# Layer 0's output product: its first half as seven block products

## The chip, the cores and the metric

The kernel runs on 1 core of one Trainium2 chip. The metric is the device time of one execution in microseconds (us). Before the change it is 828.9 us, the median of 3 runs (828.73 to 829.05). The profiled execution took 828.51 us, with a span of 826.8 us from its first to its last instruction.

## The reference, cut to what matters

Four residual layers over a sequence of 256 positions and 1024 channels, in float32. Layers 0 and 3 are mixer A:

```
def mixer_a(h, w_in, v_gain, w_s, b_s, w_out):
    proj = h @ w_in
    u = proj[..., :A_WIDTH]
    v = rms_norm(proj[..., A_WIDTH:2 * A_WIDTH], v_gain)
    z = proj[..., 2 * A_WIDTH:]
...
    mixed = jnp.einsum('gij,bcjgd->bcigd', ws, v) + b_s.T[None, None, :, :, None]
...
    y = u * mixed * jax.nn.silu(z)
    return y @ w_out
```

`A_WIDTH` is 2048, so `y` is 256 x 2048 and `w_out` is 2048 x 1024. Layer 1 is dilated attention, layer 2 multi-scale pooling. Each layer computes `x = x + mixer(rms_norm(x))`.

## The kernel before

**Three passes per product.** Every operand of a large product is a pair of float32r tiles, a rounded high part and the remainder as low part. `mm3` (L85) issues high x high, high x low and low x high, so three matmuls stand for one product. ScalarE rounds (`hi_of`, L91), VectorE subtracts (`lo_of`, L94).

**The weight stream.** All weights are one list of units of 128 x 1024 floats (two k-blocks of 128 rows by 512 columns, 512 KB). A unit is loaded by SyncE's queue into a raw buffer (`load_units`, tiles wr, wx, wy, xs), split by ScalarE (tile w48h for unit 48) and VectorE (w48l), and used by TensorE. Seven split pairs exist; in most stages the split of unit u+5 is written into the program while unit u is multiplied (`step` with AHEAD = 5). A raw buffer is loaded again as soon as VectorE has lowered its unit. An ordinary unit is used for both halves t = 0, 1 of the 256 positions: 2 k-blocks x 2 x 3 passes = 12 matmuls of 512 columns.

**Order.** Work beside the products is written as generators that `tick` advances; one tick passes per k-block, so two per ordinary unit. The order in which the generators emit is the program order of each engine, and each engine runs in that order. The numbers after `spawn(` and `yield` are delays in ticks.

**Layer 0** (`layer_a`): products v0 to v3 (units 0 to 15), then for n = 0 to 3 the products z (four units) and u (four units), units 16 to 47. After u of n, `y_task` multiplies on VectorE (L669 to L674), TensorE transposes y of each t (`yp`, L682) through one PSUM bank, ScalarE and VectorE split it into y0nh and y0nl. There is one `yp` bank, so the transposes of t = 1 start when VectorE has lowered those of t = 0. Then `proj_out` (L522) multiplies y by units 48 to 63 into four PSUM banks wo and adds them to x. In the figures below, unit 48 is the first unit of this output product.

**Seven products in layer 3.** Three of layer 3's z/u blocks (`SEVEN`) are already computed as seven block products after Strassen and Winograd in place of eight. Sums of weight quarters that this needs are made by POOL's DMA queue in DRAM (`sums_of_quarters`: copies at L188, accumulating transfers at L186), 16 transfers per block, spread over layers 0, 1 and 2; `JOBS = (19, 16)` says how many of the 48 are issued in layers 0 and 1. Sums of the left operand's quarters are made on VectorE (`sums_task`, L694). A product of this kind uses two units, each with one t only: 6 matmuls of 512 columns per unit (`product`, L720). The seven products' results are kept by ScalarE (`keep`, `minus`) and combined by VectorE.

**Next layer's constants.** `load_b` (L810) loads layer 1's masks and tables on POOL's queue into kcb, when layer 0's spatial weights are done with that tile, and 20 ticks later multiplies four small tables on VectorE (L827).

Of the kernel before, what the change touches and what calls it, by code (L numbers as in the profile page):

```python
# [17 lines left out]
P = 128  # L18
# [25 lines left out]
LAST_AHEAD = 3  # L44
WARM = 17
FILL = 4
SEVEN = (0, 2, 3)
JOBS = (19, 16)


@with_exitstack
def hybrid_trunk_kernel(ctx, tc, x, wts, norm_gainT, a_v_gain, a_wsT, a_bsT, b_gl, b_gv, c_scaleT,
# [92 lines left out]
    sums = {(n, j): dp.tile([4, P, UNIT], F32, name=f"sums{n}{j}") for n in SEVEN for j in range(2)}

    def seven_units(n):

        return n_units - 48 + 8 * n + (8 if n == 3 else 0)

    for n in reversed(SEVEN):
        z = seven_units(n)
        seq[z:z + 8] = [e[j] for e in (((n, 0, 0), (n, 0, 1)), (z, z + 1), (z + 6, z + 7), ((n, 3, 0), (n, 3, 1)),
                                       (z + 2, z + 3), ((n, 2, 0), (n, 2, 1)), ((n, 1, 0), (n, 1, 1)))
                        for j in range(2)]
    n_seq = len(seq)

    raw_users = {"wr": [-1] * RAW_BUFS, "xs": [-1], "wx": [-1], "wy": [-1]}

    def raw_place(i):  # L160

        return ("wr", "wr", "wx", "wr", "wy", "wr", "xs")[i % 7] if i >= n_units - 48 else "wr"

    def load_free():

# [22 lines left out]
                nc.gpsimd.dma_start(dst, src, max_dma_last_dim=UNIT)  # L188
            yield every

    def sum_jobs(n):

        z = seven_units(n)
        both = range(2)
        jobs = [(sums[n, j][i], wts[z + 2 * q + j], add) for i, q, add in
                ((0, 0, False), (2, 2, False), (0, 2, True), (2, 3, True)) for j in both]
        jobs += [(sums[n, j][3], sums[n, j][0], False) for j in both]
        jobs += [(sums[n, j][1], wts[z + 2 + j], False) for j in both]  # L200
        jobs += [(sums[n, j][3], wts[z + 6 + j], True) for j in both]
        jobs += [(sums[n, j][1], sums[n, j][3], True) for j in both]
# [319 lines left out]
    def proj_out(layer, nkt, yT, k0=0):  # L522


        acc = [[[(slice(0, HALF), pp(f"wo{layer}_{t}{n}"))] for n in range(2)] for t in range(2)]
        if layer == DEPTH - 1:

            acc[1][1] = [(slice(0, S), acc[1][1][0][1][:, :S]), (slice(S, HALF), atp(f"wo{layer}_b")[:, :S])]
        jt = (nkt - TAIL) // 2
        for j in range(k0 // 2, jt):  # L530
            for n in range(2):
                w = next_unit()
                for kk in range(2):
# [54 lines left out]
    def layer_a(layer, consts, pl, mid):  # L588
# [98 lines left out]
                    yield 1  # L687
            done.add(("y", layer, n))


        if layer == DEPTH - 1:
            smh, sml = pair(pl, [P, 4, 4, P], "sm", f"sm{layer}", 1)

        def sums_task():  # L694
            q = {}
            for k, t in ((1, 1), (0, 1), (0, 0), (1, 0)):
                d = q[k, t] = tmp("sz", f"sq{layer}{k}{t}", 4).rearrange("p (k c) -> p k c", c=P)
                hh, hl = (a[:, 4 * k:4 * k + 4, t * P:(t + 1) * P].bitcast(F32) for a in hcur)
                nc.vector.tensor_tensor(d, hh, hl, op=ALU.add)
                yield 1  # L700
            a11, a12, a21, a22 = q[0, 0], q[1, 0], q[0, 1], q[1, 1]
            for i, (d, a, b, op) in enumerate(((a22, a21, a22, ALU.subtract), (a21, a11, a21, ALU.subtract),
                                               (a11, a22, a11, ALU.subtract), (a12, a12, a11, ALU.add))):
                nc.vector.tensor_tensor(d, a, b, op=op)
                hi_of(smh[:, i], d)
                yield 1
                lo_of(sml[:, i], d, smh[:, i])
                yield 1
            done.add(("sums", layer))

        S_A21_A22, S_A11_A21, S_REST, S_A12_REST = range(4)

        def seven_products(n):

            need(("sums", layer))

            def sm(i):
                return lambda k: (smh[:, i, k], sml[:, i, k])

            def product(o, a, first):  # L720
                for j in range(2):
                    w = next_unit()
                    for kk in range(2):
                        k = 2 * j + kk
                        mm3(o, a(k), (w[0][:, kk], w[1][:, kk]), first and k == 0, k == 3)
                        step(kk, due=kk == 1)
# [104 lines left out]
    def layer_b(layer, consts, pl):  # L831
# [247 lines left out]
    def layer_c(layer, pl):  # L1079
# [285 lines left out]
```

## Time and profile before

| what | value |
| --- | --- |
| median of 3 runs | 828.9 us |
| the profiled execution, its span | 828.51 us, 826.8 us |
| TensorE (PE) busy | 821.1 us, 99% |
| VectorE (DVE) busy | 581.4 us, 70% |
| ScalarE (ACT) busy | 514.9 us, 62% |
| GpSimd (POOL) busy | 83.5 us, 10% |
| layer 0, products z and u | 51.7 to 147.4 us |
| layer 0, output product | 147.4 to 190.7 us |

Matmuls are pipelined: each is shown with 0.39 us, while the next one starts sooner, so a busy TensorE is not one at its peak, and the distance from start to start is the cost of a matmul. For VectorE too the distance of two starts is what an instruction takes in a full queue.

### The profile page before, as it was taken

How to read it: one execution, taken by the hardware profiler on the slowest of the kernel's cores; microseconds unless marked ns; L12 is line 12 of the kernel's file. 1: busy time of each engine (PE TensorE's matmuls, PEld its weight loads, DVE VectorE, ACT ScalarE, POOL GpSimd, SP SyncE). 2: the span in 40 equal slices, each digit the busy share in tenths (PEclk: the TensorE clock that was granted, in tenths of full speed). 3: DMA queues.
4: the chain of work that ended last, by engine and by line, in shares of the span. 5: the costliest groups of instructions: out<-in, count | busy, mean ns of one | idle time of the engine just before them, and what ended most of it. 6: DMA issues, size and time to landing. Idle time of an engine off the chain costs nothing.

```text
span 826.8 us, 12566 instructions
## 1 busy us (share of the span) xinstructions
PE 821.1 (99%) x4585; PEld 711.4 (86%) x4585; DVE 581.4 (70%) x958; ACT 514.9 (62%) x947; POOL 83.5 (10%) x117
## 2 busy tenths in 40 slices
PE   9999999999999999999999999999999999999998
PEld 7888888888988888888888889999988888888887
DVE  5876656646657667667668576897864799979692
ACT  7775444436668687688688567546643668656560
POOL 1113120000201021021011014020000000000000
PEclk9999999999999999999999999999999999999999
DMA  8879999562968357369447269999665378868661
GB/s 281 305 241 311 322 319 300 176 197 84 288 201 228 125 194 242 125 164 250 147 149 257 78 200 280 291 279 278 231 227 178 103 244 303 289 213 324 200 234 52
DMA packets 60895, 184.21 MB, mean 223 GB/s; under 512 B 5952, under 2 KB 19024, under 8 KB 60704
## 3 DMA queue, kind: packets, MB, share of 16 engines
q1 hardware_dynamic: 43440, 154.16, 53.9%
q0 software_dynamic: 17104, 28.96, 15.4%
q8 instruction: 36, 0.59, 0.3%
q10 hardware_dynamic: 288, 0.28, 0.1%
q14 instruction: 27, 0.22, 0.1%
HBM read 182.32 MB, written 26.21 MB: 252 GB/s over the span
## 4 chain that ended last, share of the span: by engine, by line
PE 97%; DVE 1%; DMA 1%; ACT 1%; issue 0%; POOL 0%; ACTq 0%
PE qk L87 5%; PE qk L89 5%; PE qk L88 5%; PE wo L87 5%; PE wo L89 5%; PE wo L88 5%; PE v L87 5%; PE v L89 5%; PE v L88 5%; PE z L89 2%; PE z L87 2%; PE u L87 2%; PE u L88 2%; PE z L88 2%; PE u L89 2%; PE cz L89 2%
## 5 line engine op out<-in xcount | busy, mean ns | idle before, releaser
L854 POOL TENSOR_TENSOR qr<-qm,m 128x8 f32<-128x8 f32 x12 | 19.9, 1658 | 215.4 <-DVE qm L853 215.4
L849 ACT ACTIVATE junk<-qk 128x128 bf16<-128x128 f32 x96 | 26.6, 277 | 7.3 <-PE qk L89 4.7
L858 ACT ACTIVATE qn<-qk,qr 128x128 f32<-128x128 f32 x96 | 27.5, 381 | 3.6 <-POOL qr L854 3.6
L307 POOL TENSOR_TENSOR r<-ms,m 128x1 f32<-128x1 f32 x6 | 4.3, 710 | 198.5 <-DVE ms L304 198.5
L325 ACT ACTIVATE hT<-hp,gT 128x128 fp32r<-128x128 f32 x48 | 13.0, 383 | 15.0 <-PE hp L321 15.0
L186 POOL DMA_DIRECT2D sums<-in_wts_dram x18 | 19.3, 1205 | 24.1 <-DMA sums<-in_wts_dram 13.1
L853 DVE TENSOR_SCALAR qm<-qs 128x8 f32<-128x8 f32 x12 | 2.1, 172 | 26.7 <-ACT junk L849 26.7
L551 DVE TENSOR_TENSOR x<-wo,x 128x512 f32<-128x512 f32 (+1 forms) x16 | 10.8, 672 | 13.4 <-PE wo L89 13.3
L849 ACT ACTIVATION_READ_ACCUMULATOR junk<-qk 128x1 f32 x96 | 18.9, 197 | 0.0
L330 DVE SCALAR_TENSOR_TENSOR hT<-hp,gT,hT 128x128 fp32r<-128x128 f32 x48 | 13.5, 343 | 7.4 <-ACT hT L325 7.4
L299 ACT ACTIVATE junk<-x 128x512 bf16<-128x512 f32 x16 | 10.2, 639 | 10.1 <-DVE x L551 9.9
L948 ACT ACTIVATE p<-p,rl 128x384 f32<-128x384 f32 (+1 forms) x16 | 11.5, 769 | 4.8 <-DVE rl L947 4.8
L879 PE MATMUL qt<-ident,qn 128*128 128x128 f32 x96 | 14.4, 272 | 0.0
L871 DVE TENSOR_TENSOR rb<-qn,kcb 128x32 f32<-128x32 f32 x96 | 13.7, 184 | 0.0
L879 PEld LDWEIGHTS qt<-ident,qn 128*128 128x128 f32 x96 | 11.7, 140 | 2.3
L607 DVE TENSOR_TENSOR vv<-v,kc 128x512 f32<-128x512 f32 x16 | 10.7, 686 | 4.0 <-ACT junk L605 3.7
L669 DVE SCALAR_TENSOR_TENSOR sz<-u,m,sz 128x512 f32<-128x512 f32 x8 | 6.0, 746 | 10.3 <-PE u L89 10.3
L944 ACT ACTIVATE p<-p,nb 128x768 f32<-128x768 f32 x8 | 7.5, 937 | 7.6 <-DVE nb L943 7.6
L188 POOL DMA_DIRECT2D sums<-in_wts_dram x18 | 12.1, 716 | 0.3 <-issue 0.3
L867 DVE TENSOR_TENSOR ra<-qn,kcb 128x64 f32<-128x64 f32 x48 | 10.6, 220 | 1.1 <-ACT qn L858 0.4
L626 POOL TENSOR_TENSOR vr<-vme,m 128x1 f32<-128x1 f32 x4 | 2.8, 716 | 73.5 <-DVE vms L622 73.5
L979 PE MATMUL pt<-ident,p 128*128 128x128 f32 x48 | 9.9, 274 | 0.0
(2965 smaller groups left out, 3359.3 us busy)
## 6 DMA issues: line engine op xcount, KB each, us to landing
wr<-in_wts_dram SPq DMA_DIRECT2D x251, 512.0 KB, 4.6
sums<-in_wts_dram POOLq DMA_DIRECT2D x36, 512.0 KB, 11.8
wr<-sums SPq DMA_DIRECT2D x19, 512.0 KB, 4.6
sums<-sums POOLq DMA_DIRECT2D x12, 512.0 KB, 8.5
wx<-in_wts_dram SPq DMA_DIRECT2D x7, 512.0 KB, 5.1
wy<-in_wts_dram SPq DMA_DIRECT2D x7, 512.0 KB, 5.3
wx<-sums SPq DMA_DIRECT2D x3, 512.0 KB, 5.4
kc<-in_a_wsT_dram POOLq DMA_DIRECT2D x2, 512.0 KB, 7.6
```

The lines of the kernel that those rows point to most:

```text
L87: nc.tensor.matmul(out_ap, lh[0], rh[0], start=start, stop=False, skip_group_check=True)
L88: nc.tensor.matmul(out_ap, lh[0], rh[1], start=False, stop=False, skip_group_check=True)
L89: nc.tensor.matmul(out_ap, lh[1], rh[0], start=False, stop=stop, skip_group_check=True)
L186: nc.gpsimd.dma_start(dst, src, accum_op=ALU.add, max_dma_last_dim=UNIT)
L188: nc.gpsimd.dma_start(dst, src, max_dma_last_dim=UNIT)
L325: nc.scalar.activation(h_parts(layer)[0][:, k, t * P:(t + 1) * P], pt[:, k % 4], AF.Copy, scale=gT[:, layer, k:k + 1])
L330: nc.vector.scalar_tensor_tensor(hTl, pt[:, k % 4], gT[:, layer, k:k + 1], hTh.bitcast(F32), op0=ALU.mult, op1=ALU.subtract)
L849: nc.scalar.activation(junk[:, :HD], ov[t][:, h], AF.Square, accum_out=ssq[t][:, h:h + 1])
L854: nc.gpsimd.tensor_tensor(rqs, ms, m05_row[:, :8], op=ALU.pow)
L858: nc.scalar.activation(qn[t][:, h], ov[t][:, h], AF.Copy, scale=rq[t][:, h:h + 1])
L871: nc.vector.tensor_tensor(rb[:, hs, s0:s0 + 16], qn[t][:, hs, s1:s1 + 16], c, op=ALU.mult)
L879: nc.tensor.transpose(pts[t][:, h], qn[t][:, h], ident)
```

## The change

**The block products.** The first 8 of the 16 units of layer 0's output product (y's blocks 0 and 1, that is k-blocks 0 to 7) become seven block products of two units: 14 units of 6 matmuls (units 48 to 61) in place of 8 units of 12. The other half stays as it was (units 62 to 69). The seven results go into banks xw, yw, zw, ww and are added to x straight from PSUM by VectorE, seven adds of 128 x 512 (`add`). Banks xw and zw collect more than one product: xw is added to x after its first product, then takes the second, is subtracted, takes the third, is subtracted and added; zw is added, takes a second product, is added again. So each later product of a bank waits for the add before it.

**The sums.** Four sums of weight quarters come from 16 more transfers on POOL's queue, 64 in all: 19 in layer 0, 24 in layer 1, 21 in layer 2. Layer 0's begin with this block and are written into the program before `load_b`. Four sums of y's quarters are made by VectorE (`left_sums`) during z and u of n = 2, in the idle tiles wx and wy, and split by both engines: 8 adds, 4 roundings, 4 subtractions.

**The postponed parts.** In layer 0 the transposes of y come 4 ticks after `y_task`'s products in place of 2, and `load_b` starts 48 ticks later.

```diff
-SEVEN = (0, 2, 3)
-JOBS = (19, 16)
+BLOCKS = {("wo", 0): 48, ("zu", 0): -48, ("zu", 2): -32, ("zu", 3): -16}
+JOBS = (19, 24)
...
+        order = (3, 0, 2, 6, 1, 5, 4) if b[0] == "zu" else (0, 1, 3, 6, 2, 5, 4)
+        seq[z:z + 8] = [quarters[q][j] for q in order for j in range(2)]
...
+        return ("wr", "wr", "xs", "wr", "wr", "wx", "wy")[(i - out_raw) % 7] if out_raw <= i < out_raw + 14 else "wr"
...
+    def part_product(o, a, first):
+
+        for j in range(2):
+            w = next_unit()
+            for kk in range(2):
+                k = 2 * j + kk
+                mm3(o, a(k), (w[0][:, kk], w[1][:, kk]), first and k == 0, k == 3)
+                step(kk, due=kk == 1)
...
+    def proj_seven(layer, yT, smh, sml):
+
+
+        def add(t, n, o, op=ALU.add):
+            xh = xt[t][:, n * HALF:(n + 1) * HALF]
+            nc.vector.tensor_tensor(xh, xh, o, op=op)
+            yield 1
...
+        xb = pp(f"xw{layer}")
+        part_product(xb, quarter(0, 0), True)
+        spawn(add(0, 0, xb), 1)
+        yb = pp(f"yw{layer}")
+        part_product(yb, quarter(1, 0), True)
+        spawn(add(0, 0, yb), 1)
+        need(("sums", layer))
+        zb = pp(f"zw{layer}")
+        part_product(zb, sum_tile(smh, sml, S_A21_A22), True)
+        spawn(add(1, 1, zb), 1)
+        part_product(xb, sum_tile(smh, sml, S_REST), False)
+        spawn(add(0, 1, xb, ALU.subtract), 1)
+        part_product(zb, sum_tile(smh, sml, S_A12_REST), False)
+        spawn(add(0, 1, zb), 1)
+        part_product(xb, sum_tile(smh, sml, S_A11_A21), False)
+        spawn(add(1, 1, xb, ALU.subtract), 1)
+        spawn(add(1, 0, xb), 1)
+        wb = pp(f"ww{layer}")
+        part_product(wb, quarter(1, 1), True)
+        spawn(add(1, 0, wb), 1)
...
+            if layer == 0 and n == 0:
+                spawn(sums_of_quarters(jobs[:JOBS[0]], 3, 29))
...
-        if layer == 0:
-            spawn(sums_of_quarters(jobs[:JOBS[0]], 4, 6))
+        def y_sums():
+
+            while ("y", layer, 1) not in done:
+                yield 1
+            room = [wx[:, 0], wx[:, 1], wy[:, 0], wy[:, 1]]
...
+            if n == 2 and ("wo", layer) in BLOCKS:
+                spawn(y_sums(), 4)
...
-            spawn(y_task(n, proj_tok(f"u{layer}{n}"), us))
-
-        proj_out(layer, 16, get, KT if layer == DEPTH - 1 else 0)
+            spawn(y_task(n, proj_tok(f"u{layer}{n}"), us, 4 if late(layer) else 2))
+
+        if ("wo", layer) in BLOCKS:
+            proj_seven(layer, get, smh, sml)
+        proj_out(layer, 16, get, KT if layer == DEPTH - 1 or ("wo", layer) in BLOCKS else 0)
...
-                    spawn(sums_of_quarters(jobs[JOBS[0]:sum(JOBS)], 10, 5))
+                    spawn(sums_of_quarters(jobs[JOBS[0]:sum(JOBS)], 7, 5))
...
-        spawn(sums_of_quarters(jobs[sum(JOBS):], 7, 4))
+        spawn(sums_of_quarters(jobs[sum(JOBS):], 5, 4))
...
-        spawn(load_b())
+        spawn(load_b(), 48)
```

The order of the instructions moves on VectorE at three places. The first is the stretch of layer 0 from n = 2 on, up to the lowering of y's block 2 for t = 0 (y02l). VectorE, before:

```order
L95 TENSOR_TENSOR w39l<-wr_944,w39h 128x1024
L95 TENSOR_TENSOR w40l<-wr_962,w40h 128x1024
L95 TENSOR_TENSOR w41l<-wr_999,w41h 128x1024
L95 TENSOR_TENSOR w42l<-wr_1024,w42h 128x1024
L95 TENSOR_TENSOR w43l<-wr_1044,w43h 128x1024
L95 TENSOR_TENSOR w44l<-wr_1062,w44h 128x1024
L669 SCALAR_TENSOR_TENSOR sz_1064<-u_0_1068,m_77,sz_1064 128x512
L674 SCALAR_TENSOR_TENSOR yy_1160<-mx_1104,bs_267,sz_1064 128x256 x2
L669 SCALAR_TENSOR_TENSOR sz_1066<-u_1_1069,m_77,sz_1066 128x512
L674 SCALAR_TENSOR_TENSOR yy_1164<-mx_1111,bs_267,sz_1066 128x256 x2
L95 TENSOR_TENSOR w45l<-wr_1087,w45h 128x1024
L95 TENSOR_TENSOR y02l<-yp_1186,y02h 128x4x128
```

VectorE, changed, the end of the same stretch (sm0h and sm0l are the parts of the sums of y's quarters):

```order
L605 TENSOR_TENSOR wx<-wy,wx 128x512
L97 TENSOR_TENSOR sm0l<-wx,sm0h 128x512
L97 TENSOR_TENSOR w44l<-wr_1061,w44h 128x1024
L752 SCALAR_TENSOR_TENSOR sz_1063<-u_0_1067,m_79,sz_1063 128x512
L757 SCALAR_TENSOR_TENSOR yy_1171<-mx_1109,bs_269,sz_1063 128x256 x2
L752 SCALAR_TENSOR_TENSOR sz_1065<-u_1_1068,m_79,sz_1065 128x512
L757 SCALAR_TENSOR_TENSOR yy_1175<-mx_1116,bs_269,sz_1065 128x256 x2
L605 TENSOR_TENSOR wx<-wx 128x512
L97 TENSOR_TENSOR sm0l<-wx,sm0h 128x512
L97 TENSOR_TENSOR w45l<-wr_1088,w45h 128x1024
L97 TENSOR_TENSOR w46l<-wr_1124,w46h 128x1024
L97 TENSOR_TENSOR y02l<-yp_1220,y02h 128x4x128
```

The eight adds and four lowerings of the sums now stand between y01l and y02l, two of them and w46l between the products of y and y02l.

The second place is the start of the output product. VectorE, before, after the last products of y:

```order
L95 TENSOR_TENSOR w53l<-wr_1281,w53h 128x1024
L95 TENSOR_TENSOR y03l<-yp_1382,y03h 128x4x128
L95 TENSOR_TENSOR w54l<-wr_1313,w54h 128x1024
L95 TENSOR_TENSOR y03l<-yp_1407,y03h 128x4x128
L95 TENSOR_TENSOR w55l<-wr_1332,w55h 128x1024
L95 TENSOR_TENSOR w56l<-wr_1350,w56h 128x1024
```

VectorE, changed, at the same place (x<-x,xw is the add of a product to x):

```order
L97 TENSOR_TENSOR w53l<-wx,w53h 128x1024
L97 TENSOR_TENSOR w54l<-wy,w54h 128x1024
L629 TENSOR_TENSOR x<-x,xw_1386 128x512
L97 TENSOR_TENSOR w55l<-wr_1281,w55h 128x1024
L97 TENSOR_TENSOR w56l<-wr_1305,w56h 128x1024
L97 TENSOR_TENSOR y03l<-yp_1432,y03h 128x4x128
L629 TENSOR_TENSOR x<-x,yw_1409 128x512
L97 TENSOR_TENSOR w57l<-wr_1338,w57h 128x1024
L97 TENSOR_TENSOR w58l<-wr_1356,w58h 128x1024
L97 TENSOR_TENSOR y03l<-yp_1463,y03h 128x4x128
L629 TENSOR_TENSOR x<-x,zw_1441 128x512
L97 TENSOR_TENSOR w59l<-wr_1374,w59h 128x1024
```

The adds of the products now stand among the splits; a unit here means half as many matmuls as before.

The third place is the end of the seven products, units 61 to 66. VectorE, before:

```order
L95 TENSOR_TENSOR w61l<-wr_1471,w61h 128x1024
L95 TENSOR_TENSOR w62l<-wr_1489,w62h 128x1024
L95 TENSOR_TENSOR w63l<-wr_1508,w63h 128x1024
L95 TENSOR_TENSOR w64l<-wr_1526,w64h 128x1024
L95 TENSOR_TENSOR w65l<-wr_1544,w65h 128x1024
L95 TENSOR_TENSOR w66l<-wr_1562,w66h 128x1024
```

VectorE, changed:

```order
L97 TENSOR_TENSOR w61l<-wy,w61h 128x1024
L97 TENSOR_TENSOR w62l<-wr_1421,w62h 128x1024
L905 TENSOR_TENSOR kcb<-kcb 128x192 x4
L629 TENSOR_TENSOR x<-x,zw_1441 128x512
L97 TENSOR_TENSOR w63l<-wr_1439,w63h 128x1024
L97 TENSOR_TENSOR w64l<-wr_1470,w64h 128x1024
L629 TENSOR_TENSOR x<-x,xw_1386 128x512 x2
L97 TENSOR_TENSOR w65l<-wr_1484,w65h 128x1024
L97 TENSOR_TENSOR w66l<-wr_1517,w66h 128x1024
L629 TENSOR_TENSOR x<-x,ww_1548 128x512
```

The four table products of the next layer (kcb) and four adds have come in. The last add, x<-x,ww, frees the bank that the ordinary products take for wo_11, from the second group of three matmuls of unit 63 on.

More of the change, by code (lines that the diff above doesn't have):

```diff
@@ L144, in hybrid_trunk_kernel, with first_of @@
     seq = list(range(n_units))
[L145 to L155, printed above, removed]
+    sums = {(b, j): dp.tile([4, P, UNIT], F32, name=f"sums{b[0]}{b[1]}{j}") for b in BLOCKS for j in range(2)}
+    def first_of(b):
+        return BLOCKS[b] % n_units
+    for b in sorted(BLOCKS, key=first_of, reverse=True):
+        z = first_of(b)
+        quarters = [(z, z + 1), (z + 2, z + 3), (z + 6, z + 7)] + [((b, i, 0), (b, i, 1)) for i in range(4)]
+        order = (3, 0, 2, 6, 1, 5, 4) if b[0] == "zu" else (0, 1, 3, 6, 2, 5, 4)
+        seq[z:z + 8] = [quarters[q][j] for q in order for j in range(2)]
     n_seq = len(seq)
+    more_raw = seq.index((("zu", 0), 0, 0))
+    out_raw = first_of(("wo", 0))
     raw_users = {"wr": [-1] * RAW_BUFS, "xs": [-1], "wx": [-1], "wy": [-1]}
     def raw_place(i):
-        return ("wr", "wr", "wx", "wr", "wy", "wr", "xs")[i % 7] if i >= n_units - 48 else "wr"
+        if i >= more_raw:
+            return ("wr", "wr", "wx", "wr", "wy", "wr", "xs")[(i - more_raw) % 7]
+        return ("wr", "wr", "xs", "wr", "wr", "wx", "wy")[(i - out_raw) % 7] if out_raw <= i < out_raw + 14 else "wr"
     def load_free():
@@ L189, in sums_of_quarters, with sum_jobs @@
             yield every
-    def sum_jobs(n):
-        z = seven_units(n)
+    def sum_jobs(b):
+        z = first_of(b)
         both = range(2)
-        jobs = [(sums[n, j][i], wts[z + 2 * q + j], add) for i, q, add in
+        jobs = [(sums[b, j][i], wts[z + 2 * q + j], add) for i, q, add in
                 ((0, 0, False), (2, 2, False), (0, 2, True), (2, 3, True)) for j in both]
[L199 to L202, printed above, removed]
+        jobs += [(sums[b, j][3], sums[b, j][0], False) for j in both]
+        jobs += [(sums[b, j][1], wts[z + 2 + j], False) for j in both]
+        jobs += [(sums[b, j][3], wts[z + 6 + j], True) for j in both]
+        jobs += [(sums[b, j][1], sums[b, j][3], True) for j in both]
         return jobs
@@ L522, in proj_out, with bank @@
     def proj_out(layer, nkt, yT, k0=0):
-        acc = [[[(slice(0, HALF), pp(f"wo{layer}_{t}{n}"))] for n in range(2)] for t in range(2)]
+        acc = [[[], []], [[], []]]
+        def bank(t, n):
+            if not acc[t][n]:
+                acc[t][n].append((slice(0, HALF), pp(f"wo{layer}_{t}{n}")))
+        if ("wo", layer) not in BLOCKS:
+            for t in range(2):
+                for n in range(2):
+                    bank(t, n)
         if layer == DEPTH - 1:
@@ L535, in proj_out @@
                     for t in range(2):
+                        bank(t, n)
                         for cs, o in acc[t][n]:
@@ L571, in proj_out, with left_sums @@
                 tick()
+    S_A21_A22, S_A11_A21, S_REST, S_A12_REST = range(4)
+    def left_sums(name, quarter, place, smh, sml, key):
+        q = {}
+        for k, t in ((1, 1), (0, 1), (0, 0), (1, 0)):
+            d = q[k, t] = place(f"sq{name}{k}{t}").rearrange("p (k c) -> p k c", c=P)
+            hh, hl = (a.bitcast(F32) for a in quarter(k, t))
+            nc.vector.tensor_tensor(d, hh, hl, op=ALU.add)
+            yield 1
+        a11, a12, a21, a22 = q[0, 0], q[1, 0], q[0, 1], q[1, 1]
+        for i, (d, a, b, op) in enumerate(((a22, a21, a22, ALU.subtract), (a21, a11, a21, ALU.subtract),
+                                           (a11, a22, a11, ALU.subtract), (a12, a12, a11, ALU.add))):
+            nc.vector.tensor_tensor(d, a, b, op=op)
+            hi_of(smh[:, i], d)
+            yield 1
+            lo_of(sml[:, i], d, smh[:, i])
+            yield 1
+        done.add(key)
@@ L688, in y_task, with h_quarter @@
             done.add(("y", layer, n))
-        if layer == DEPTH - 1:
+        if layer == DEPTH - 1 or ("wo", layer) in BLOCKS:
             smh, sml = pair(pl, [P, 4, 4, P], "sm", f"sm{layer}", 1)
[L694 to L711, printed above, removed]
+        def h_quarter(k, t):
+            return (a[:, 4 * k:4 * k + 4, t * P:(t + 1) * P] for a in hcur)
         def seven_products(n):
@@ L717, in sm @@
             def sm(i):
[L718 to L726, printed above, removed]
+                return sum_tile(smh, sml, i)
+            product = part_product
             def minus(o, name):
@@ L788, in get, with place, y_quarter @@
             return yT[k // 4][0][:, k % 4, sl], yT[k // 4][1][:, k % 4, sl]
-        if layer == 0:
-            spawn(sums_of_quarters(jobs[:JOBS[0]], 4, 6))
+        def y_sums():
+            while ("y", layer, 1) not in done:
+                yield 1
+            room = [wx[:, 0], wx[:, 1], wy[:, 0], wy[:, 1]]
+            def place(name):
+                return room.pop()
+            def y_quarter(k, t):
+                return (a[:, :, t * P:(t + 1) * P] for a in yT[k])
+            yield from left_sums(layer, y_quarter, place, smh, sml, ("sums", layer))
         for n in range(4):
+            if n == 2 and ("wo", layer) in BLOCKS:
+                spawn(y_sums(), 4)
             if layer == DEPTH - 1 and n == 3:
                 proj_half(layer, KT, get)
-            if layer == DEPTH - 1 and n in SEVEN:
+            if layer == DEPTH - 1 and ("zu", n) in BLOCKS:
                 seven_products(n)
@@ L1208, in hybrid_trunk_kernel @@
     box = {}
-    jobs = [e for n in SEVEN for e in sum_jobs(n)]
+    jobs = [e for b in BLOCKS for e in sum_jobs(b)]
     def after_ws():
-        spawn(load_b())
+        spawn(load_b(), 48)
     with tc.tile_pool(name="L0", bufs=1, reuse_waits="tile") as pl:
```

9 lines of the change are left out of this document (8 added, 1 removed).

## The prediction
> **What bounds the kernel now.** I read the page first: the busy shares, then the chain of work that ended last by engine.
>
> ```profile
> PE 821.1 (99%) x4585; PEld 711.4 (86%) x4585; DVE 581.4 (70%) x958; ACT 514.9 (62%) x947; POOL 83.5 (10%) x117
> PE 97%; DVE 1%; DMA 1%; ACT 1%; issue 0%; POOL 0%; ACTq 0%
> ```
>
> TensorE is on the chain for 97%. Next the view of waits for TensorE alone, all of its rows (total, times, longest):
>
> ```profile
> PE warm L291 <- DVE wx L65: 1.1, 1, 1.1
> PE hp L321 <- DVE xs L315: 0.5, 1, 0.5
> PE v L429 <- ACT hT L404: 0.3, 1, 0.3
> PE xb L87 <- ACT n L730: 0.3, 1, 0.3
> ```
>
> TensorE waits 2.2 us in all, nowhere in the stages that change. Then busy times by stage (span, then PE, PEld, DVE, ACT, POOL, granted clock, DMA share, GB/s); the rows are n = 2, n = 3 and the output product of layer 0:
>
> ```profile
> 98.50:123.00 24.50, 24.50 (x119) 20.51 (x118) 14.29 (x17) 10.49 (x12) 5.54 (x7) 1.00 1.10 332
> 123.00:147.40 24.40, 24.40 (x118) 20.41 (x118) 14.20 (x17) 10.49 (x12) 0.46 (x1) 1.00 0.90 288
> 147.40:190.70 43.30, 43.30 (x197) 35.77 (x197) 24.16 (x28) 17.05 (x20) 0.56 (x1) 1.00 0.53 170
> ```
>
> TensorE is full at granted clock 1.00; VectorE has 10 us free in n = 2 and 19 us in the output product. So a matmul removed is time removed, while VectorE keeps up with what is put on it.
>
> **Removed: 12 matmuls.** TensorE's timeline from u into the output product:
>
> ```profile
> 146.77 0.39 PE L87 MATMUL u<-w47h,hT 128*128 128x512 f32 x1
> ...
> 149.94 0.39 PE L89 MATMUL wo<-w48h,y00l 128*128 128x512 f32 x1
> ```
>
> These are the first and the last of 15 starts, so a matmul costs 3.17 / 14 = 0.2264 us. 8 units x 12 = 96 matmuls become 14 x 6 = 84: **-2.72 us**. An ordinary unit lasts 2.72 us, a seven-product unit 1.36.
>
> **What VectorE's additions cost.** Its timeline in a full queue (layer 3's first block):
>
> ```profile
> 697.09 1.22 DVE L95 TENSOR_TENSOR w232l<-wr,w232h 128x1024 fp32r<-128x1024 f32 x1
> 698.22 1.22 DVE L95 TENSOR_TENSOR w233l<-wx,w233h 128x1024 fp32r<-128x1024 f32 x1
> ...
> 707.43 0.68 DVE L758 TENSOR_TENSOR p<-yb,p 128x512 f32<-128x512 f32 x1
> 708.03 1.22 DVE L95 TENSOR_TENSOR w239l<-wr,w239h 128x1024 fp32r<-128x1024 f32 x1
> ```
>
> From start to start a split takes 1.14 us, an operation on 512 columns 0.60; the last of a queue ends 1.22 or 0.69 after its start. So each starts 0.08 or 0.09 before the one ahead of it is shown to end; that without this overlap VectorE would be later is the last rival. [...]
>
> The multiplication of y, the four table products, and the round trips with ScalarE are shown by these:
>
> ```profile
> 146.97 0.75 DVE L669 SCALAR_TENSOR_TENSOR sz<-u,m,sz 128x512 f32<-128x512 f32 x1 [3.90 <-PE u L89]
> ...
> 150.12 1.22 DVE L95 TENSOR_TENSOR w53l<-wr,w53h 128x1024 fp32r<-128x1024 f32 x1
> 151.44 0.69 DVE L95 TENSOR_TENSOR y03l<-yp,y03h 128x512 fp32r<-128x512 f32 x1
> 152.39 1.22 DVE L95 TENSOR_TENSOR w54l<-wr,w54h 128x1024 fp32r<-128x1024 f32 x1 [0.26 <-ACT w54h L92]
> ```
>
> ```profile
> 89.75 1.16 DVE L827 TENSOR_TENSOR kcb<-kcb 128x192 f32<-128x192 f32 x4
> 90.82 1.22 DVE L95 TENSOR_TENSOR w34l<-wr,w34h 128x1024 fp32r<-128x1024 f32 x1
> ```
>
> ```profile
> 658.32 0.69 DVE L607 TENSOR_TENSOR vv<-v,kc 128x512 f32<-128x512 f32 x1 [0.73 <-ACT junk L605]
> 658.92 1.48 DVE L95 TENSOR_TENSOR v30l<-vv,v30h 128x512 fp32r<-128x512 f32 x2
> 659.04 0.63 ACT L92 ACTIVATE v30h<-vv 128x512 fp32r<-128x512 f32 x1 [0.24 <-DVE vv L607]
> ```
>
> The products of y take 3.15 us, the tables 1.07. An operation, its rounding on ScalarE and its lowering take 1.39 us from start to start: 658.32 to the second lowering, which starts 0.69 before its end at 660.40. A split behind a lowering that waited for ScalarE starts 0.95 later (151.44 to 152.39), since ScalarE rounds in turn. So one sum of quarters with the split behind it costs 1.39 + 0.95 + 1.14 = 3.48 us.
>
> **Wait A: y's sums hold the second transposes of n = 2.** They start when y's block 1 is lowered, and the transposes of t = 1 need y02l of t = 0 behind them.
>
> ```profile
> 106.28 0.69 DVE L95 TENSOR_TENSOR y01l<-yp,y01h 128x512 fp32r<-128x512 f32 x1 [1.04 <-ACT y01h L92]
> ```
>
> ```profile
> 129.20 0.60 PE L682 MATMUL yp<-ident,yy 128*128 128x128 f32 x4
> ```
>
> Both move 2 ticks, one ordinary unit, later: y01l ends at 109.69, the transposes would start at 131.92. VectorE's queue between: four adds and two splits (2.40 + 2.28, to 114.4), three sums with a split (10.44, to 124.85), the products of y (3.15, to 128.0), the fourth sum with a split (3.48, to 131.5), w46l (1.14), y02l (0.69): 133.3. TensorE waits **1.4 us**. Postponing moves both ends alike, so it saves nothing here. Behind this wait in TensorE's queue stands only z, whose units are ready. The bounds are 0, if VectorE finds 1.4 us, and 2.7, if the 15 operations that follow another without a round trip each took their full 1.22 or 0.69 before the next starts (15 x 0.085 = 1.3).
>
> **Wait B: the last add frees a bank too late.** Count from TensorE's start of unit 48, where the products of y begin at -0.48 as before (147.45 against 146.97). Ahead of x<-x,ww stand, by the order: the products of y 3.15, the 14 splits w53l to w66l 15.96, seven adds 4.20, two lowerings of y 1.20, the tables 1.07, in sum 25.58. So x<-x,ww runs from 25.10 to 25.79. TensorE would need its bank after 14 units (19.02), two groups of transposes, unit 62 (2.72) and three matmuls (0.68). What transposes and a restart after a wait cost:
>
> ```profile
> 125.76 0.39 PE L89 MATMUL z<-w40h,hT 128*128 128x512 f32 x1
> 125.99 0.60 PE L682 MATMUL yp<-ident,yy 128*128 128x128 f32 x4
> 126.34 0.48 PE L87 MATMUL z<-w41h,hT 128*128 128x512 f32 x1
> 126.66 0.40 PE L88 MATMUL z<-w41l,hT 128*128 128x512 f32 x1
> ```
>
> ```profile
> 703.46 0.39 PE L89 MATMUL yb<-w233h,hT 128*128 128x512 f32 x1
> 704.11 0.50 PE L87 MATMUL xb<-w234h,sm3h 128*128 128x512 f32 x1 [0.27 <-ACT n L730]
> 704.44 0.39 PE L88 MATMUL xb<-w234l,sm3h 128*128 128x512 f32 x1
> ```
>
> Transposes add 0.45 (125.76 to 126.66 is 0.90 for two matmul steps of 0.45), a restart 0.10. So the need is at 23.32, and TensorE loses 25.79 - 23.32 + 0.10 = **2.6 us**. Part falls earlier: x<-x,zw ends at 12.6, and unit 56 needs that bank at 11.8; but the end is set by VectorE's queue alone, so earlier waits are inside the 2.6. The bounds are 0 and 4.6 (2.6, and 0.085 on some 24 operations). Behind the waiting matmul stand only the ordinary units; VectorE catches up there at 1.14 us of work per 2.72.
>
> **Edits at nothing.** Six more splits on ScalarE: it is busy 17.05 of 43.3 us above. Sixteen more transfers: layers 1 and 2 carried 29, now 45, and TensorE waited for none; bounded by one blocking POOL ahead of a norm for the 10.62 us it once waited, which five units of split weights (13.6 us) cover:
>
> ```profile
> 104.86 1.05 POOL L186 DMA_DIRECT2D sums<-in_wts_dram  x1 [10.62 <-DMA sums<-sums]
> ...
> 120.55 1.00 POOL L186 DMA_DIRECT2D sums<-sums  x1 [3.91 <-issue]
> ```
>
> `load_b` loads later, but 20 ticks still lie between it and the tables; without its transfers ahead the sums come sooner.
>
> **Sum.** 828.51 (profiled) - 2.72 + 1.4 + 2.6 = 829.8; on the median, 0.4 higher, 828.9 + 1.3 = 830.2. A comparison here can tell 0.2%, 1.7 us.
>
> **Rivals.**
>
> *The waits do not come (faster).* Layer 3's blocks have as full a VectorE, 23.32 of 24.00 and 21.98 of 23.00 us, and TensorE idles 0.27 and 0:
>
> ```profile
> 690.00:714.00 24.00, 23.73 (x110) 19.42 (x109) 23.32 (x27) 19.88 (x27) 1.73 (x2) 1.00 0.91 314
> 734.00:757.00 23.00, 23.00 (x112) 19.27 (x111) 21.98 (x25) 16.20 (x20) 0.00 (x0) 1.00 0.76 275
> ```
>
> With their worst loss (0.42 + 0.11 at 704) it is 828.9 - 2.72 + 0.53 = 826.7. Against it: there ScalarE frees the banks, here VectorE does, behind the splits. 14 in 100.
>
> *Late weights make wait B longer (slower).* w66's buffer is free when w62l ends at 17.75; a median landing and a split on ScalarE make it 17.75 + 4.6 + 1.06 = 23.4, and VectorE reaches w66l at 23.96.
>
> ```profile
> wr<-in_wts_dram SPq DMA_DIRECT2D x251, 512.0 KB, 4.6
> ```
>
> ```profile
> ACT w28h L92 <- DMA wr<-in_wts_dram: 5.0, 1, 5.0
> ```
>
> Beyond a landing of 5.2 us each microsecond is lost; ScalarE once waited 5.0 for one, among POOL's transfers. With 2 us late: 832.2. 12 in 100.
>
> *The sums come late.* SyncE's queue reaches them with w52 near 137 and holds all loads behind. Before, the first block's last transfer was issued at 120.55, and load_b's transfers no longer stand ahead of it. Ten microseconds late, less 6.8 of ready units, gives 833.4. 3 in 100.
>
> *VectorE's operations do not overlap.* Wait A grows by 1.3 and B by 2.0, their upper bounds: 833.5. Against it: the starts above. 2 in 100.
>
> **How the numbers follow.** 69 in 100 for the forecast, 829 to 831.4; about 47 of these within 0.2% (to 830.6), 22 above. With the rivals: faster 0.14, same 0.47, slower 0.39. The range, 826.7 to 832.3, takes in the rivals of both signs up to their central cases, and so the bounds from no waits to a late weight; both waits at their upper bounds lie outside.
>
> **What would show it.** Right: TensorE's waits list yp <- DVE y02l near 132 us with 1 to 1.5, and wo <- DVE x near 173 with 1 to 2, zw before it with under 1; VectorE without a gap from the products of y to x<-x,ww; matmuls 0.2264 apart elsewhere; from 200 us on a constant offset. Wrong: no wait at these places (then the bank or the queue was misread), waits on weights or sums instead, or a new wait in layers 1 and 2.

## The result and the profile after

| | median us | range of the executions, us | ratio to before, 95% interval |
| --- | --- | --- | --- |
| before | 828.61 (10 runs) | 828.46 to 829.05 | |
| changed | 832.26 (10 runs) | 829.77 to 834.92 | 1.0044 [1.0028, 1.0061] |

The changed kernel is slower, by more than the 0.2% that can be told. The forecast was 830.2 with a range up to 832.3. Two things stand side by side: the profiled execution is the lowest of the ten, and its own time, 829.77 us, is the forecast sum of 829.8; but the other nine lie up to 5.2 us above it, where before varied by 0.6 us. So the sum was right for the execution that the trace shows, and a cost is missing that this trace does not show. That the median of 832.26 still lies inside the range is luck: the range reaches 832.3 because of a weight 2 us late in layer 0's output product, and the experiments show that this is not what happened. (One disturbed execution of an experiment below, sum_later, took 1019.62 us at a granted clock of 0.753 and is left out of its range.)

The page's busy times, and then all waits of TensorE in the changed kernel (total, times, longest):

```profile
PE 819.6 (99%) x4573; PEld 708.6 (86%) x4573; DVE 600.3 (72%) x984; ACT 523.9 (63%) x957; POOL 99.5 (12%) x133
```

```profile
PE yp L765 <- DVE y02l L97: 1.2, 1, 1.2
PE warm L298 <- DVE wx L67: 1.1, 1, 1.1
PE wo L89 <- DVE x L629: 1.1, 1, 1.1
PE zw L89 <- DVE x L629: 0.7, 1, 0.7
PE hp L328 <- DVE xs L322: 0.5, 1, 0.5
PE xb L89 <- ACT n L790: 0.3, 1, 0.3
```

Twelve matmuls fewer, and three new waits, at the places that were forecast. Below is wait A in TensorE's timeline, and VectorE's queue at that place (its first and its last row):

```profile
131.60 0.39 PE L91 MATMUL z<-w42h,hT 128*128 128x512 f32 x1
133.24 0.66 PE L765 MATMUL yp<-ident,yy 128*128 128x128 f32 x4 [1.25 <-DVE y02l L97]
```

```profile
108.91 0.69 DVE L97 TENSOR_TENSOR y01l<-yp,y01h 128x512 fp32r<-128x512 f32 x1 [1.02 <-ACT y01h L94]
...
132.50 0.68 DVE L97 TENSOR_TENSOR y02l<-yp,y02h 128x512 fp32r<-128x512 f32 x1
```

The transposes could have started at 131.60 + 0.23 = 131.83; they start at 133.24, so TensorE loses 1.41 us. Wait B follows, first VectorE's queue from the products of y to the last add (its first and its last row, with no gap between them in the trace), then TensorE at the bank that this add frees:

```profile
148.35 0.75 DVE L752 SCALAR_TENSOR_TENSOR sz<-u,m,sz 128x512 f32<-128x512 f32 x1 [3.90 <-PE u L91]
...
173.85 0.68 DVE L629 TENSOR_TENSOR x<-x,ww 128x512 f32<-128x512 f32 x1
```

```profile
173.12 0.39 PE L91 MATMUL wo<-w63h,y02l 128*128 128x512 f32 x1
174.58 0.50 PE L89 MATMUL wo<-w63h,y02h 128*128 128x512 f32 x1 [1.07 <-DVE x L629]
174.91 0.40 PE L90 MATMUL wo<-w63l,y02h 128*128 128x512 f32 x1
```

VectorE works from 148.35 to 174.53, 26.18 us, where the working had 26.27 (0.48 ahead of the start of unit 48 and 25.79 behind it). Eight adds to x run there, not the seven that the description of the change names; seven of them stand ahead of the last one, as the sum had it. TensorE loses 174.58 - 173.12 - 0.23 = 1.23 us and 0.1 at the restart; the wait for zw before it is shown with 0.7.

What remains of all this at the start of layer 1, before and after, in TensorE's timelines:

```profile
197.75 0.48 PE L87 MATMUL qk<-w67h,hT 128*128 128x512 f32 x1
```

```profile
198.88 0.47 PE L89 MATMUL qk<-w73h,hT 128*128 128x512 f32 x1
```

The same unit starts 1.13 us later, although 2.72 us of matmuls are gone, so the two waits cost 1.13 + 2.72 = 3.85 us; 4.0 was forecast.

### The profile page after: what moved, and what is told of

The parts are those of the page before. It is cut to its first block, busy times and chain, and to the rows that moved or that the text cites. A ratio compares the mean times of both kernels' runs of the same rounds, so it can differ in the third digit from the quotient of the medians.

```text
span 828.1 us, 12625 instructions
## 1 busy us (share of the span) xinstructions
PE 819.6 (99%) x4573; PEld 708.6 (86%) x4573; DVE 600.3 (72%) x984; ACT 523.9 (63%) x957; POOL 99.5 (12%) x133
## 4 chain that ended last, share of the span: by engine, by line
PE 92%; DVE 4%; issue 2%; ACT 1%; DMA 0%; POOL 0%; DVEq 0%; ACTq 0%
PE qk L91 5%; PE qk L89 5%; PE qk L90 5%; PE v L89 5%; PE v L91 5%; PE v L90 5%; PE wo L89 4%; PE wo L91 4%; PE wo L90 4%; PE cz L91 2%; PE z L91 2%; PE z L89 2%; PE cz L89 2%; PE cz L90 2%; PE z L90 2%; PE cx L89 2%
## 5 line engine op out<-in xcount | busy, mean ns | idle before, releaser
L193 POOL DMA_DIRECT2D sumszu<-in_wts_dram x18 | 19.2, 1163 | 10.9 <-DMA sumszu<-sumszu 7.6
L195 POOL DMA_DIRECT2D sumszu<-in_wts_dram x18 | 13.0, 747 | 0.3 <-issue 0.3
L765 PE MATMUL yp<-ident,yy 128*128 128x128 f32 x64 | 9.7, 273 | 1.3 <-DVE y02l L97 1.2
L765 PEld LDWEIGHTS yp<-ident,yy 128*128 128x128 f32 x64 | 7.7, 139 | 3.6 <-DVE y02l L97 1.7
```

Of the source, the lines that this page charges most:

```text
L193: nc.gpsimd.dma_start(dst, src, accum_op=ALU.add, max_dma_last_dim=UNIT)
L765: nc.tensor.transpose(pt[:, k], ys[t][:, k * P:(k + 1) * P], ident)
```

## The experiments

Theory 1 was the rival of late weights, in the place where it was forecast: a weight that lands late in layer 0's output product makes VectorE late for x<-x,ww, and so lengthens wait B in some executions. Theory 2 was that the 64 transfers of sums, costed at nothing, do it somewhere else. Each kernel was timed beside the kernel before: 828.66 us in the first four, 828.60 in the next four, 828.70 in the last three. The middle four (sums_earlier to all_and_ahead) ran on another chip than the other seven. The kernel before takes the same time on both to 0.1 us, but a spread is compared safely only between kernels that ran on the same chip.

**again.** The changed kernel, no edit.

> The changed kernel once more, for the spread of its executions (829.8 to 834.9 us, where before has 828.5 to 829.1) and for the trace of another execution. Theory 1 (a weight late for VectorE lengthens wait B): a slower execution shows wo <- DVE x longer than 1.1 us, ScalarE waiting for w66's landing longer than 2.9 us ahead of it, and all else as in the first trace. Theory 2 (the sums' transfers): a slower execution shows TensorE behind POOL's blocked queue in layers 1 and 2, or waiting for sm0 or a sumswo weight near 137 us. Median 832 by both; if the profiled execution is a fast one, it decides nothing.

Median 830.64 us (829.87 to 834.42, 11 runs), ratio 1.0032 [1.0022, 1.0043]. The profiled execution took 830.18 and has the same waits to 0.1 us, so it decides nothing, as said. Over both sets 8 of 21 executions are above 832 us.

**wwbank.** The last product in a bank of another tag:

```diff
-        wb = pp(f"ww{layer}")
+        wb = atp(f"ww{layer}")
```

> The last product's bank ww is taken from the three banks of the mixing, two of which are idle then; no instruction changes place. The ordinary products no longer wait for x<-x,ww. Theory 1 (wait B is that bank, and a late weight ahead of that add makes the spread): wo <- DVE x goes from the waits, an execution like the profiled one takes 828.6 us (829.8 - 1.2), the median falls by 2.5 to 3.5 us to about 829, and the spread to under 1.5 us. Theory 2 (the spread is the sums' transfers in layers 1 and 2): the wait goes, the median falls by 1.2 us only, to 831, and the spread stays at 5 us.

Median 829.06 (828.47 to 830.71, 11 runs), ratio 1.0008 [0.9999, 1.0016]. The wait of wo is gone from the list, zw stays at 0.7; the lowest execution fell by 1.4 us against again. So this bank is what TensorE waited for. The median is the "about 829" of theory 1, but it fell by only 1.6 us against again; the spread of 2.2 us lies between the theories. Together they decide for neither.

**load_b_early.**

```diff
-        spawn(load_b(), 48)
+        spawn(load_b())
```

> The next layer's constants load undelayed, as before the change: their transfers and the four table products move ahead of the output product. If the four table products (1.07 us) in VectorE's queue are part of wait B, wo <- DVE x falls by 1.1 to about 0 and an execution like the profiled one takes 828.7; if the constants' transfers crowd the sums (they stand ahead of them on POOL's queue), the sums come 4 us later, and it costs nothing as long as they land before 134 us. If the delay only moved the work elsewhere in a full queue: no change beyond 0.5 us.

Median 829.85 (828.73 to 834.44, 12 runs), ratio 1.002 [1.0009, 1.0031]. The lowest fell by 1.1 us, the 1.07 of the four table products: they are part of wait B. And the profiled execution was the highest of its twelve, so it shows what the first trace did not. Its longest waits of TensorE, and TensorE's timeline there, in layer 2's output product:

```profile
PE wo L89 <- DVE cyy L1251: 2.4, 1, 2.4
...
PE qt L957 <- DVE qk00l L965: 1.2, 1, 1.2
```

```profile
605.15 0.39 PE L91 MATMUL wo<-w198h,cy3l 128*128 128x512 f32 x1
607.90 0.68 PE L89 MATMUL wo<-w199h,cy3h 128*128 128x512 f32 x1 [2.36 <-DVE cyy L1251]
608.38 0.63 PE L90 MATMUL wo<-w199l,cy3h 128*128 128x512 f32 x1
608.81 0.63 PE L91 MATMUL wo<-w199h,cy3l 128*128 128x512 f32 x1
...
611.37 0.45 PE L91 MATMUL wo<-w199h,cy3l 128*128 128x512 f32 x1
611.65 0.39 PE L89 MATMUL wo<-w199h,cy3h 128*128 128x512 f32 x1
```

VectorE and ScalarE ahead of it:

```profile
605.83 1.23 DVE L97 TENSOR_TENSOR w202l<-wr,w202h 128x1024 fp32r<-128x1024 f32 x1 [1.46 <-ACT w202h L94]
606.98 1.66 DVE L1251 SCALAR_TENSOR_TENSOR cyy<-cg,csc,szT 128x256 f32<-128x256 f32 x4
```

```profile
602.06 1.06 ACT L94 ACTIVATE w201h<-wr 128x1024 fp32r<-128x1024 f32 x1 [1.21 <-DMA wr<-in_wts_dram]
604.74 1.06 ACT L94 ACTIVATE w202h<-wr 128x1024 fp32r<-128x1024 f32 x1 [1.62 <-DMA wr<-in_wts_dram]
```

Read from the bottom: ScalarE waits for weights to land, w201 and then w202. VectorE, in order, waits for the rounding of w202 and only then reads the bank cg into cyy. TensorE needs that bank for the second unit of the output product. It is the mechanism of the rival with late weights, a bank freed behind a late split, but 430 us later than I had placed it.

How near the other executions were to it: the same read of the bank and TensorE's start of the same unit, before (VectorE, TensorE),

```profile
600.55 1.66 DVE L1173 SCALAR_TENSOR_TENSOR cyy<-cg,csc,szT 128x256 f32<-128x256 f32 x4 [1.05 <-PE cg L89]
```

```profile
603.84 0.39 PE L87 MATMUL wo<-w193h,cy3h 128*128 128x512 f32 x1
```

and in the first trace of the changed kernel:

```profile
603.62 1.65 DVE L1251 SCALAR_TENSOR_TENSOR cyy<-cg,csc,szT 128x256 f32<-128x256 f32 x4
```

```profile
604.97 0.39 PE L89 MATMUL wo<-w199h,cy3h 128*128 128x512 f32 x1
```

Before, VectorE starts 3.29 us ahead of TensorE and has waited only for TensorE itself; now it starts 1.35 us ahead. Why the weights land later is in two views, of the windows around it (before, then changed; the last three numbers are granted clock, DMA share, GB/s), and of the DMA issues of 560 to 605 us with their median time to landing (before, then changed):

```profile
560.00:575.00 15.00, 15.00 (x132) 15.00 (x131) 11.42 (x16) 8.72 (x12) 1.23 (x2) 1.00 1.09 292
575.00:590.00 15.00, 15.00 (x132) 15.00 (x131) 14.21 (x23) 9.62 (x13) 0.00 (x0) 1.00 0.69 237
```

```profile
575.00:590.00 15.00, 15.00 (x132) 15.00 (x131) 12.46 (x20) 9.03 (x11) 1.02 (x1) 1.00 1.12 312
```

```profile
wr<-in_wts_dram SPq DMA_DIRECT2D x18, 512.0 KB, 4.8
sums<-sums POOLq DMA_DIRECT2D x2, 512.0 KB, 10.2
```

```profile
wr<-in_wts_dram SPq DMA_DIRECT2D x18, 512.0 KB, 6.5
sumszu<-in_wts_dram POOLq DMA_DIRECT2D x4, 512.0 KB, 14.2
sumszu<-sumszu POOLq DMA_DIRECT2D x2, 512.0 KB, 11.0
```

Before, the DMA engines were full up to about 575 us; now they stay full for 15 us longer, and a weight takes 6.5 us in place of 4.8. The Trainium skill, page "DMA: Bandwidth & Descriptors", section "Issuing engines are not separate DMA queues", says that transfers from all issuing engines run on the same 16 DMA engines and interleave; these rows agree. From here on theory 2 reads: 21 transfers of sums in layer 2, where before had 13, delay its weights.

**wait_2.** The transposes 2 ticks after the products, as before:

```diff
-            spawn(y_task(n, proj_tok(f"u{layer}{n}"), us, 4 if late(layer) else 2))
+            spawn(y_task(n, proj_tok(f"u{layer}{n}"), us, 2))
```

> The transposes of y come 2 ticks after the products again, as before the change. My step said that postponing moves both ends alike, so wait A does not change: yp <- DVE y02l stays at 1.0 to 1.5 us, and the time within 0.5 us of the changed kernel. If postponing did gain, wait A grows towards 2.7 us or y03's lowering comes to stop the output product, and the time rises by 1 us or more.

Median 831.29 (829.98 to 835.9, 10 runs), ratio 1.0042 [1.0027, 1.0057]; the lowest is 0.1 us above again's. The wait only shows at the first transposes, behind the products of y, instead of the second:

```profile
PE yp L765 <- DVE yy L757: 0.8, 1, 0.8
```

In its timeline the two transposes start 1.00 and 0.29 us late (gaps of 1.23 and 0.52 us where 0.23 is the distance of two matmuls), 1.29 in place of 1.41. With the restarts, units 40 to 43 take 13.29 us from start to start here, 13.30 in the changed kernel and 11.85 before. Postponing is worth nothing here, as forecast. (The median is 0.65 us above again's, a little more than the 0.5 that was allowed; this spread can't tell that from nothing.)

**sums_earlier.** Eight of layer 2's transfers in layer 1:

```diff
-JOBS = (19, 24)
+JOBS = (19, 32)
...
-                    spawn(sums_of_quarters(jobs[JOBS[0]:sum(JOBS)], 7, 5))
+                    spawn(sums_of_quarters(jobs[JOBS[0]:sum(JOBS)], 5, 5))
...
-        spawn(sums_of_quarters(jobs[sum(JOBS):], 5, 4))
+        spawn(sums_of_quarters(jobs[sum(JOBS):], 7, 4))
```

> Eight of layer 2's 21 transfers of sums are issued in layer 1 (19, 32, 13 in layers 0, 1, 2, as many in layer 2 as before the change); nothing else moves. Theory 2 (the spread is the weight stream of layer 2, late beside the transfers that now run until about 595 us): the DMA share of 575 to 590 us falls from 1.12 to about 0.7, TensorE's start of layer 2's second output unit comes without a wait in every execution, the fast executions stay at 829.8, the slowest falls from 834.4 to under 831, the median to 829.9. Theory 1 (the spread is a late weight in the output product of layer 0): spread and median stay, 830.6 and up to 834. If layer 1 can't bear 32, a new wait for qt or a weight shows between 200 and 480 us.

Median 830.24 (830.02 to 831.55, 9 runs), ratio 1.0025 [1.0015, 1.0034]. No execution is above 832 us, and the median is the 830.2 of the forecast. The window, where about 0.7 was expected:

```profile
575.00:590.00 15.00, 15.00 (x132) 15.00 (x131) 14.31 (x24) 9.87 (x14) 0.00 (x0) 1.00 0.81 255
```

The top was expected under 831 and is 831.55: something of 1.3 us is left. A candidate is the wait for qt at the start of layer 1 in load_b_early's list, with 1.2 us; that list's own execution is not this one, so it stays a candidate.

**sum_later.** The last sum of y's quarters 4 ticks later:

```diff
+            if layer_wait and i == 3:
+                yield 4
             nc.vector.tensor_tensor(d, a, b, op=op)
             hi_of(smh[:, i], d)
```

> The last of the four sums of y's quarters is made 4 ticks later, so that it and its split stand behind y02l on VectorE. Wait A is VectorE's queue between y01l and y02l, so 3.48 us less in it removes the 1.2 to 1.4 us: yp <- DVE y02l goes, zw <- x and wo <- x stay within 0.3 us of 0.7 and 1.1 (their queue starts at the products of y behind u of n = 3), and a fast execution takes 828.4 instead of 829.8; the spread stays. If the wait moves on to the second transposes of n = 3 or to w53, the time doesn't fall.

Median 829.28 (828.44 to 832.33, 11 of its executions), ratio 1.0011 [1.0002, 1.0019]. The lowest is where it was expected: yp <- y02l is gone, wo and zw stand at 1.1 and 0.7, and the spread stays. Its profiled execution (830.21) shows the candidate again:

```profile
PE qt L959 <- DVE qk00l L967: 1.0, 1, 1.0
```

**earlier_bank_later.** wwbank, sums_earlier and sum_later in one.

> Three edits together: transfers of sums as in sums_earlier, bank of the last product as in wwbank, last sum of y as in sum_later. If the three costs add up (wait A 1.4, wait B's last part 1.2, the spread), 827.2 in fast executions and at most 1 us of spread: median 827.4, 1.2 us faster than before the change. If waits A and B feed one another (TensorE earlier by 1.4 reaches the zw bank earlier), the zw wait grows by part of it and the median is 828 to 828.6.

Median 827.30 (826.97 to 829.04, 11 runs), ratio 0.9986 [0.9977, 0.9994]. By the median the three costs add up (827.4 was expected). The spread of 2.1 us is not the 1 us that was expected at most: two executions, 828.25 and 829.04, lie higher.

**all_and_ahead.** The same, and splits 4 units ahead in the seven products, so that VectorE comes to each add one split sooner:

```diff
-    def part_product(o, a, first):
+    def part_product(o, a, first, ahead=AHEAD):
...
-                step(kk, due=kk == 1)
+                step(kk, ahead, due=kk == 1)
...
-        part_product(xb, quarter(0, 0), True)
+        part_product(xb, quarter(0, 0), True, 4)
```

> As earlier_bank_later, and in the seven products the splits are written 4 units ahead in place of 5, so each add to x stands one split (1.14 us) earlier on VectorE and the zw wait of 0.7 (0.85 with the restart) should go: 826.4 in fast executions, median 826.6. If the splits then come late, waits on w..l of DVE show at units 56 to 62 or the buffers come free later and the end of the output product waits instead, at the norm's transposes (hp) by about 1 us, and it is no faster than earlier_bank_later.

Median 826.43 (826.03 to 826.77, 7 runs), ratio 0.9973 [0.9963, 0.9984]: faster than before the change. All waits of TensorE:

```profile
PE warm L298 <- DVE wx L67: 1.1, 1, 1.1
PE hp L328 <- DVE xs L322: 0.5, 1, 0.5
PE xb L89 <- ACT n L792: 0.3, 1, 0.3
```

No wait of the change is left, and the feared one at the norm did not come. Of the 2.72 us that the matmuls are worth, 2.2 arrive.

**before_21.** The control: the kernel before, with nothing but its transfers of sums moved.

```diff
-JOBS = (19, 16)
+JOBS = (19, 8)
...
-        spawn(sums_of_quarters(jobs[sum(JOBS):], 7, 4))
+        spawn(sums_of_quarters(jobs[sum(JOBS):], 5, 4))
```

> The kernel before, with eight of its 48 transfers of sums moved from layer 1 to layer 2 (19, 8, 21 in place of 19, 16, 13; one every 5 ticks there), the same 21 as in the changed kernel; no seven products in layer 0, no other edit. Theory 2 (21 transfers in layer 2 make the weight stream late): DMA share 1.1 in the 15 us where before has 0.69, and executions from 828.5 up to 833 where before stays under 829.3; median 829 to 831. Theory 1 or any cause in layer 0's new products: 828.6 with a spread under 1 us.

Median 830.82 (829.73 to 832.16, 8 runs), ratio 1.0026 [1.0016, 1.0037]. The first row of its waits of TensorE, and the window:

```profile
PE wo L87 <- DVE cyy L1173: 1.9, 1, 1.9
```

```profile
575.00:590.00 15.00, 15.00 (x133) 15.00 (x132) 12.68 (x18) 8.68 (x11) 1.01 (x1) 1.00 1.12 311
```

Without any of the new products the kernel loses 2.1 us in the median and spreads over 2.4 us, on the same chip as again; even its lowest execution is 1.3 us above before's. So the moved transfers are enough for such a loss and such a spread, and neither needs layer 0's new products. Their number and their pace (one every 5 ticks in place of 7) were moved together and are not told apart.

**all_but_sums.** all_and_ahead with the changed kernel's 19, 24, 21 transfers.

> all_and_ahead with the transfers of sums as in the changed kernel (19, 24, 21): the waits of layer 0 are gone, the sums of layer 2 are late again. If the two causes stand apart: fast executions 826.2, and slow ones up to 831; median 827 to 829. If the moved transfers did nothing and all_and_ahead owes its small spread to layer 0's edits: as all_and_ahead, 826.4 with a spread of 0.7.

Median 827.20 (826.54 to 831.79, 11 runs), ratio 0.9987 [0.9976, 0.9997]. The spread is back to 5 us with layer 0 free of waits, and the list shows wo <- DVE cyy with 0.6. The two causes stand apart, though all_and_ahead with its spread of 0.7 us ran on the other chip. Only one of eleven is more than 2.2 us above the lowest, so the spread's size is not a fixed number.

**sums_29.** The changed kernel with 16 transfers in layer 1 and 29 in layer 2:

```diff
-JOBS = (19, 24)
+JOBS = (19, 16)
...
-                    spawn(sums_of_quarters(jobs[JOBS[0]:sum(JOBS)], 7, 5))
+                    spawn(sums_of_quarters(jobs[JOBS[0]:sum(JOBS)], 10, 5))
...
-        spawn(sums_of_quarters(jobs[sum(JOBS):], 5, 4))
+        spawn(sums_of_quarters(jobs[sum(JOBS):], 4, 4))
```

> The changed kernel with 29 transfers of sums in layer 2 and 16 in layer 1 (one every 4 ticks in layer 2). If the time is lost to layer 2's weights beside the transfers, more of them lose more and lose it in nearly every execution: wo <- DVE cyy of 1 to 3 us in the profile, fast executions over 831, median 833 to 836. If their number there doesn't matter, as again: 829.9 to 834.4 with a median near 831.

Median 836.05 (835.26 to 838.07, 4 runs), ratio 1.0096 [1.0081, 1.0112]. Its waits in layer 2:

```profile
PE wo L89 <- DVE cyy L1251: 2.6, 1, 2.6
...
PE wo L89 <- ACT szT L1193: 0.6, 1, 0.6
```

More transfers there cost more, now in every execution, and the median is just above the 833 to 836 expected. The list also has 0.5 us for qt in layer 1 and 0.6 for zb in layer 3, so not all of the 5.4 us above again is layer 2's.

**All profiled executions at this place.** In each trace, this is the time from TensorE's first matmul of layer 2's first output unit (w198; w192 in before and before_21) to its first matmul of the third (w200; w194). It is two ordinary units, 5.44 us by the working:

| transfers of sums in layer 2 | us in each trace |
| --- | --- |
| 13 | before 5.48; sums_earlier, earlier_bank_later and all_and_ahead 5.49 each |
| 21 | changed and wait_2 5.49; again 5.81; wwbank 5.91; sum_later 6.04; all_but_sums 6.47; before_21 7.78; load_b_early 9.73 |
| 29 | sums_29 8.57 |

With 13 transfers none of four executions loses time here; with 21 six of eight lose 0.3 to 4.2 us, on both chips. Even again's trace, whose list shows nothing new, loses 0.33 us here, most of the 0.41 us by which it is slower than the changed kernel's first trace. So the place and the cause do not rest on the one high execution alone.

## Why the prediction was right, and where it was not

- **Removed matmuls, 2.72 us.** Right: 4585 became 4573, matmuls elsewhere keep their distance (131.60 follows 131.38), and all_and_ahead brings 2.2 us in the median once the waits are gone.
- **Wait A, 1.4 us.** Right: 1.41, with y02l at 132.50 to 133.18 where the sum had 133.3. sum_later took it away by moving 3.48 us of that queue.
- **Postponed transposes save nothing.** Right, by wait_2.
- **Wait B, 2.6 us.** Right in mechanism and nearly in size: both waits together cost 3.85 us for 4.0. Its parts were taken out one by one: the bank (wwbank, 1.4 us at the lowest execution), the tables in the queue (load_b_early, 1.1, a part of the same time), and the zw wait (all_and_ahead against earlier_bank_later, 0.9 in the medians).
- **"VectorE's operations do not overlap", "The waits do not come", "The sums come late".** None came: the waits of the list are at the places and with nearly the sizes of the forecast, and no list shows TensorE behind a sum.
- **Edits at nothing: sixteen more transfers.** This step failed, and with it the median, 2.1 us above the forecast. It reasoned that layers 1 and 2 "carried 29, now 45, and TensorE waited for none", and took as its bound what a blocked POOL could do to a norm. POOL was not the resource: the DMA engines were. In layer 2 their share was 1.09 already up to 575 us; eight more transfers keep it at 1.12 for 15 us more, a weight lands after 6.5 us in place of 4.8, and a cover of 3.29 us ahead of cyy shrinks to 1.35 or is overrun. In the changed kernel the cost is nothing at the lowest execution and up to 5.2 us at others; in before_21 the lowest already pays 1.3 us. By the medians it is 2.1 us in before_21. Between sums_earlier, whose 830.24 is the forecast, and again it is 0.4, and 2.0 to the first ten executions; but again ran on another chip than sums_earlier, and the chip of the first ten is not on record.
- **Late weights make wait B longer.** The mechanism was the right one and the place the wrong one. In layer 0 w66 did land late, but ScalarE, after 2.86 us of waiting, had rounded it by 171.04, and VectorE came to w66l at 172.71. These are the rows of the changed kernel (ScalarE, VectorE):

```profile
169.98 1.06 ACT L94 ACTIVATE w66h<-wr 128x1024 fp32r<-128x1024 f32 x1 [2.86 <-DMA wr<-in_wts_dram]
```

```profile
172.71 1.21 DVE L97 TENSOR_TENSOR w66l<-wr,w66h 128x1024 fp32r<-128x1024 f32 x1
```

  Moving eight transfers off layer 2 and leaving layer 0 as it is left no execution above 832 us, and in the one high execution with a trace (load_b_early) layer 0 shows no new wait. So nothing is left that speaks for theory 1; the high executions of the changed kernel itself have no trace.
- **"From 200 us on a constant offset".** True of the first profiled execution; again's already loses 0.33 us in layer 2.

Open: the 1 to 1.3 us that some executions of sums_earlier and sum_later still lose, perhaps at the start of layer 1; whether the number of transfers or their pace in layer 2 does it; and why eight transfers cost so unequally from one set of executions to the next (the chip may be part of it).

## What to carry to other kernels

That no engine waited for a transfer before says only that there was cover: where transfers are added or moved, look at the DMA share of the stage where they will land and at how far each bank-freeing operation runs ahead of TensorE. Put an operation that frees a bank ahead of splits that are not due yet; here that, another bank, one sum made later and eight transfers moved turned a loss of 0.4% into a gain of 0.3%. And when a change spreads the executions, put the suspected part alone into the kernel before: that control takes two lines here, and it shows whether the part is enough.

## What the runs showed of the hardware

In load_b_early the wait of 2.36 us cost more than itself: of the nine matmuls behind it eight are followed by the next only after 0.42 to 0.48 us in place of 0.23, and the window of those 3.7 us has a granted clock of 0.54:

```profile
607.90:611.60 3.70, 3.70 (x9) 2.93 (x10) 3.36 (x6) 3.55 (x5) 0.00 (x0) 0.54 0.53 152
```

The unit takes 4.44 us in place of 2.72. Waits of 1.9 us in before_21 and 2.6 us in sums_29 were followed by matmuls at a granted clock of 1.00, and the unit took 2.97 and 2.93 us. So the lowered clock cost about 1.5 us more. The Trainium skill, page "TensorE: Matmul & The Clock Gate", section "Part 1: The HAM clock gate (the "warmup" mystery)", gives the halved clock after an idle window of about 3.4 us that runs freely; the 0.43 us agree with its halved clock, but the wait here was shorter than that window, and a longer one elsewhere had no such effect. What decides it was not tried. It is probably not rare: 3.7 us at 0.54 lower the mean clock of an execution of 832 us to 0.998 (1 - 3.7 x 0.46 / 832), and, apart from the one disturbed execution, twelve show 0.997 or 0.998, all in kernels with 21 or 29 transfers in layer 2, among them three of the changed kernel's first ten (833.95, 834.21, 834.48). In the experiments the kernel before and the kernels with 13 show 0.999 or 1.000 throughout. That those others lost their clock at the same place is likely, but they have no trace.
